# Other SBUF addresses for the operands of the split-float32 matmuls of a hybrid decoder layer

## The chip, the cores and the metric

One core of one Trainium2 chip. The metric is the device time of one execution in microseconds; the median of three runs of the kernel before is 854.86 us (854.53 to 857.35).

## What is computed

A decoder layer in float32 on 256 tokens of width 1024: a SwiGLU block (FFN1), a mixer in which a Mamba-2 branch and a retention branch run side by side, a second SwiGLU block (FFN2), each with a norm and a modulation from a conditioning vector, and a last norm. Cut to what matters:

```
u = modulate(rms_norm(h, norm_ffn1_w), sh1, sc1)
h = h + 0.5 * g1 * (silu(u @ w_gate) * (u @ w_up)) @ ffn1_w_out      # 1024 -> 2 x 2816 -> 1024
u = modulate(rms_norm(h, norm_mix_w), sh2, sc2)
z, xbc, dt, q, k, v, g, gates = split(u @ mix_w_in)                  # 1024 -> 13344
h = h + g2 * (gate_s * (ssd(z, xbc, dt) @ w_br_ssd)
            + gate_r * (retention(q, k, v, g) @ w_br_ret)) @ mix_w_out
u = modulate(rms_norm(h, norm_ffn2_w), sh3, sc3)
h = h + 0.5 * g3 * (silu(u @ w_gate2) * (u @ w_up2)) @ ffn2_w_out
out = rms_norm(h, norm_final_w)
```

## The kernel before

Activations lie transposed: features on the 128 partitions, the 256 tokens along the row. Every large projection is done as three matmuls with operands that are split into two parts (`float32r`): a high part, rounded by ScalarE's cast, and a low part, which VectorE gets by subtracting the high part from the full value. `mm3` (L138 to L141) issues high x high (L139), low x high (L140) and high x low (L141) into the same PSUM sum. In nearly all of them a piece of 128 x 128 weights is loaded into TensorE and 256 tokens of an activation stream past it. Where this text says "streamed operand" it means the one that flows through, and "weights" the one that is loaded; the profile writes `proj<-uh,wh` for "uh streams past wh into proj".

The tiles by name:

- `wst` holds weights as they come from memory by DMA (four buffers of 8 KB a partition), `wh` and `wl` their high and low parts (four buffers of 4 KB each, L130 and L131 in `half`).
- `uh` and `ul` are the parts of the normed and modulated activation u: eight rows of 256 tokens, with 320 elements from row to row (`U_ROW`), and two more columns that `modulated` uses (258 columns in its matmuls).
- `s` tiles are the mixer's slots: 17 buffers of 4 KB that hold, among others, the split results of both branches, which stream past `w_br_ssd`, `w_br_ret` and `mix_w_out`.
- `ah` and `al` are the split products of a SwiGLU block, which stream past the weights of its second projection in FFN1 (`contract`).
- In the v columns of the mixer (`v_tile`) and in the last projection (`ffn2_w_out`, from L985 on) the roles are changed: activations are loaded, and `wh` and `wl` stream, with 512 columns or 256.
- The narrow projection for dt (L577 to L582) puts both parts of its weights into one `wh` buffer and loads 64 or 32 columns of it at a time.

Weights arrive on SyncE's DMA queue in the order of use. In the first phase (up to the first part of FFN1's first projection) the order of ScalarE, VectorE and TensorE is written out by hand (`manual_schedule`); in the rest the code's order stands, and a list of steps (`ORDER`) sets that of the mixer.

Where a tile lies in a partition follows from the pools: `cst`, then `wp` (wst, wh, gap, wl), then `sp` (am, g, eb, gap, uh, ul and small tiles), and after these a pool for each phase, which holds `ah` and `al` or the slots. Nothing but the sizes of what stands ahead sets an address. A tile `gap` in `wp` and one in `sp` hold no data; they only move what follows. The sizes of u's rows, of the weights' pieces and of all buffers named above are multiples of 256 bytes, so that all rows of a tile have the same address modulo 256.

## Time and profile before

| | |
|---|---|
| median of three runs | 854.86 us (854.53 to 857.35) |
| the profiled execution | 856.98 us, span 854.9 us |
| TensorE busy, weight loads busy | 842.5 us, 816.4 us |
| VectorE, ScalarE, GpSimd busy | 667.5, 519.2, 10.3 us |
| mean granted TensorE clock | 0.998 |
| moved by DMA | 193.14 MB, 226 GB/s in the mean |

Matmuls overlap: one lasts some 0.28 us from start to modelled end, while the next starts about 0.12 us after it. Their rate is read from starts, or from a count in a stretch of time, and not from the mean duration. A matmul of plain float32 stands as two records in the trace, one of `float32r` as one.

### The profile page before, as it was taken

What the parts mean: (1) busy time and instruction counts of PE and PEld (TensorE: products, weight loads), DVE (VectorE), ACT (ScalarE), POOL (GpSimd) and SP (SyncE); (2) the same over time, 40 slices, a digit from 0 to 9 for tenths busy, and PEclk for the clock granted to TensorE, in tenths of its full rate; (3) what the DMA queues carried; (4) which work ended last, traced back from release to release, by engine and by line L of the source; (5) the groups of instructions that cost most, each with busy time, mean ns of one, the idle gap of its engine ahead of it and who ended that gap; (6) DMA issues with size and microseconds to landing.
All of it is one profiled execution on the core that took longest, in us unless ns stands there. A gap on an engine that the chain in (4) does not pass through costs nothing.

```text
span 854.9 us, 16219 instructions
## 1 busy us (share of the span) xinstructions
PE 842.5 (99%) x6734; PEld 816.4 (95%) x6734; DVE 667.5 (78%) x1002; ACT 519.2 (61%) x743; POOL 10.3 (1%) x21
## 2 busy tenths in 40 slices
PE   8999999999999999999999999999999999999996
PEld 6999999999999989899999999999999999999896
DVE  6989979886989987687898777977979975455463
ACT  6665544465798686766465568765558644545342
POOL 0000000000100010000000000000000000000000
PEclk9999999999999999999999999999999999999999
DMA  9987889984595455446657662645555685455521
GB/s 371 422 316 263 289 293 349 362 321 149 203 323 195 169 210 199 142 153 227 225 180 294 247 241 105 212 183 185 212 195 201 250 311 198 150 188 176 189 89 49
DMA packets 30587, 193.14 MB, mean 226 GB/s; under 512 B 3489, under 2 KB 4129, under 8 KB 10034
## 3 DMA queue, kind: packets, MB, share of 16 engines
q1 hardware_dynamic: 28656, 186.40, 59.6%
q0 software_dynamic: 1568, 5.28, 1.9%
q8 instruction: 52, 0.85, 0.4%
q10 hardware_dynamic: 290, 0.44, 0.1%
q14 instruction: 21, 0.17, 0.1%
HBM read 191.02 MB, written 1.08 MB: 225 GB/s over the span
## 4 chain that ended last, share of the span: by engine, by line
PE 91%; issue 4%; DMA 2%; ACT 2%; DVE 1%; DVEq 0%; ACTq 0%; POOLq 0%
PE proj L139 28%; PE proj L141 27%; PE proj L140 27%; PE misc L139 1%; PE misc L141 1%; PE misc L140 1%; DMA k<-in_consts_dram 1%; DMA m<-rows 1%; PE misc L734 1%; PE misc L207 1%; PE misc L878 1%; ACT wh L130 0%; DMA h<-in_x_dram 0%; PE misc L744 0%; ACT s L171 0%
## 5 line engine op out<-in xcount | busy, mean ns | idle before, releaser
L130 ACT CAST wh<-wst 128x1024 fp32r<-128x1024 f32 (+1 forms) x263 | 273.2, 1040 | 252.7 <-PE proj L140 166.8
L131 DVE TENSOR_TENSOR wl<-wst,wh 128x1024 fp32r<-128x1024 f32 (+1 forms) x263 | 317.3, 1210 | 128.7 <-ACT wh L130 128.0
L139 PE MATMUL proj<-uh,wh 128*128 128x256 f32 (+1 forms) x1312 | 369.3, 281 | 0.0
L141 PE MATMUL proj<-uh,wl 128*128 128x256 f32 (+1 forms) x1312 | 368.0, 280 | 0.0
L140 PE MATMUL proj<-ul,wh 128*128 128x256 f32 (+1 forms) x1312 | 367.5, 280 | 0.0
L141 PEld LDWEIGHTS proj<-uh,wl 128*128 128x128 f32 x1312 | 248.2, 189 | 0.2 <-issue 0.2
L139 PEld LDWEIGHTS proj<-uh,wh 128*128 128x128 f32 x1312 | 247.1, 188 | 0.3 <-ACT wh L130 0.2
L140 PEld LDWEIGHTS proj<-ul,wh 128*128 128x128 f32 x1312 | 246.9, 188 | 0.3 <-issue 0.2
L139 PE MATMUL proj<-s,wh 128*128 128x256 f32 x320 | 90.2, 283 | 1.0 <-ACT s L800 0.8
L141 PE MATMUL proj<-s,wl 128*128 128x256 f32 x320 | 89.6, 280 | 0.0
L140 PE MATMUL proj<-s,wh 128*128 128x256 f32 x320 | 89.5, 280 | 0.0
L183 DVE SCALAR_TENSOR_TENSOR wst<-wst,cb 128x1024 f32<-128x1024 f32 x56 | 67.0, 1221 | 3.3 <-DMA wst<-in_ada_w_dram 3.3
L139 PEld LDWEIGHTS proj<-s,wh 128*128 128x128 f32 x320 | 60.0, 188 | 2.1 <-ACT s L800 1.7
L141 PEld LDWEIGHTS proj<-s,wl 128*128 128x128 f32 x320 | 60.5, 189 | 0.0
L140 PEld LDWEIGHTS proj<-s,wh 128*128 128x128 f32 x320 | 60.1, 188 | 0.0
L139 PE MATMUL proj<-ah,wh 128*128 128x256 f32 x176 | 49.5, 281 | 0.0
L140 PE MATMUL proj<-al,wh 128*128 128x256 f32 x176 | 49.4, 281 | 0.0
L141 PE MATMUL proj<-ah,wl 128*128 128x256 f32 x176 | 49.4, 281 | 0.0
L139 PE MATMUL proj<-wh,ah 128*128 128x256 f32 (+1 forms) x132 | 42.1, 319 | 0.0
L140 PE MATMUL proj<-wl,ah 128*128 128x256 f32 (+1 forms) x132 | 42.0, 318 | 0.0
L141 PE MATMUL proj<-wh,al 128*128 128x256 f32 (+1 forms) x132 | 41.8, 317 | 0.0
L163 ACT ACT_TABLE_LOAD x30 | 38.5, 1283 | 1.2 <-PEq L1040 0.7
(247 smaller groups left out, 1132.6 us busy)
## 6 DMA issues: line engine op xcount, KB each, us to landing
wst<-in_mix_w_in_dram SPq DMA_DIRECT2D x52, 1024.0 KB, 4.9
wst<-in_ffn_w_in_dram SPq DMA_DIRECT2D x43, 1024.0 KB, 6.5
wst<-in_ada_w_dram SPq DMA_DIRECT2D x28, 1024.0 KB, 6.2
wst<-in_ffn_w_out_dram SPq DMA_DIRECT2D x17, 1024.0 KB, 5.2
ada<-in_ada_w_dram SPq DMA_DIRECT2D x16, 512.0 KB, 12.2
wst<-in_w_br_ssd_dram SPq DMA_DIRECT2D x8, 1024.0 KB, 5.2
wst<-in_w_br_ret_dram SPq DMA_DIRECT2D x8, 1024.0 KB, 4.9
wst<-in_ffn_w_out_dram SPq DMA_DIRECT2D x6, 768.0 KB, 4.5
```

Source lines behind the costliest of these rows:

```text
L130: act.copy(hi, v)
L131: dve.tensor_tensor(lo, v, hi.bitcast(F32), ALU.subtract)
L139: pe.matmul(o, l[0], r[0], start=first, stop=False, skip_group_check=skip)
L140: pe.matmul(o, l[0], r[1], start=False, stop=False, skip_group_check=skip)
L141: pe.matmul(o, l[1], r[0], start=False, stop=last, skip_group_check=skip)
L163: ins = act.preload_act_table_set(name).ins
L183: dve.scalar_tensor_tensor(st[:, i, :], st[:, i, :], 1.0, cb, ALU.mult, ALU.mult, accum_out=raw[:, j, f0 + i:f0 + i + 1])
L207: pe.matmul(ps[:, :T], mean, s, start=i == 0, stop=i == len(parts) - 1)
L734: pe.matmul(py[hh * 64:hh * 64 + 64, f * T + c * P:f * T + (c + 1) * P], xd[:, c, hl * 64:hl * 64 + 64], m[c][:, hl, :], start=True, stop= ...
L878: pe.matmul(py[:, eh, :], v[:, 0, es], sc[:, :T], start=True, stop=False)
```

## The change

No instruction is added, taken away or moved. Tiles get other addresses, and two tiles are read at an offset in a larger buffer:

- a `wh` buffer has 64 elements more, and its data begin 46 elements in (`WH_AT`), or 8 elements in where it streams in the last projection (`WH_MOVING`);
- the gap ahead of `wl` shrinks from 16 to 8 elements and the gap ahead of `uh` from 48 to 40;
- `ah` and `al` of FFN2 begin 48 and 0 elements into their buffers instead of 24 and 16.

Addresses modulo 256 bytes, from the two programs' allocations:

| | before | after |
|---|---|---|
| uh, ul | 0 | 192 |
| slots | 0 | 192 |
| ah, al in FFN1 | 0 | 192 |
| wh | 96 | 24 |
| wl | 160 | 128 |
| last projection: wh, wl | 96, 160 | 128, 128 |
| last projection: ah, al | 96, 160 | 128, 128 |

Smaller tiles that come after these in a partition move along.

```diff
+WH_AT, WH_MOVING = 46, 8
...
-    for tag, n, bufs in (("am", KD, 2), ("g", KD, 2), ("eb", 4, 1), ("gap", 48, 1)):
+    for tag, n, bufs in (("am", KD, 2), ("g", KD, 2), ("eb", 4, 1), ("gap", 40, 1)):
...
-    def half(v):
+    def high_weights(at_=WH_AT):
+        t = wp.tile([P, 1024 + 64], F32R, tag="wh", name=nm("wh"), bufs=HALF_BUFS)
+        return t[:, at_:at_ + 1024]
+
+    def low_weights():
+        return wp.tile([P, 1024], F32R, tag="wl", name=nm("wl"), bufs=HALF_BUFS)
+
+    def half(v, at_=WH_AT):
         nk, n = v.shape[1], v.shape[2]
-        hi = wp.tile([P, 1024], F32R, tag="wh", name=nm("wh"), bufs=HALF_BUFS)
-        lo = wp.tile([P, 1024], F32R, tag="wl", name=nm("wl"), bufs=HALF_BUFS)
+        hi, lo = high_weights(at_), low_weights()
...
-            his = [wp.tile([P, 1024], F32R, tag="wh", name=nm("wh"), bufs=HALF_BUFS) for _ in range(2)]
+            his = [high_weights() for _ in range(2)]
             if kt == 0:
-                wp.tile([P, 16], F32, tag="gap", name="wgap")
-            los = [wp.tile([P, 1024], F32R, tag="wl", name=nm("wl"), bufs=HALF_BUFS) for _ in range(2)]
-            return his, los
+                wp.tile([P, 8], F32, tag="gap", name="wgap")
+            return his, [low_weights() for _ in range(2)]
...
-            wd = wp.tile([P, 1024], F32R, tag="wh", name=nm("wh"), bufs=HALF_BUFS)
-            wd = wd[:, :KD * 2 * NH].rearrange("p (k n) -> p k n", k=KD)
+            wd = high_weights()[:, :KD * 2 * NH].rearrange("p (k n) -> p k n", k=KD)
...
-                   .rearrange("p (f t) -> p f t", f=NF) for name, n in (("ah", 24), ("al", 16)))
+                   .rearrange("p (f t) -> p f t", f=NF) for name, n in (("ah", 48), ("al", 0)))
...
-                hvs = [half(st[:, k2:min(k2 + per // 2, kn), :]) for k2 in range(0, kn, per // 2)]
+                hvs = [half(st[:, k2:min(k2 + per // 2, kn), :], WH_MOVING) for k2 in range(0, kn, per // 2)]
```

## The prediction

> **What bounds the kernel now.** I read the page's busy times first, then its chain, then the costliest groups, then stretches of the span, and last single instructions in order of time.

> ```profile
> span 854.9 us, 16219 instructions
> PE 842.5 (99%) x6734; PEld 816.4 (95%) x6734; DVE 667.5 (78%) x1002; ACT 519.2 (61%) x743; POOL 10.3 (1%) x21
> ...
> PE 91%; issue 4%; DMA 2%; ACT 2%; DVE 1%; DVEq 0%; ACTq 0%; POOLq 0%
> ...
> L139 PE MATMUL proj<-uh,wh 128*128 128x256 f32 x1280 | 359.9, 281 | 0.0
> L139 PE MATMUL proj<-s,wh 128*128 128x256 f32 x320 | 90.2, 283 | 1.0 <-ACT s L800 0.8 <-ACT s L135 0.2
> L139 PE MATMUL proj<-ah,wh 128*128 128x256 f32 x176 | 49.5, 281 | 0.0
> L139 PE MATMUL misc<-uh,wh 128*128 128x256 f32 x64 | 18.0, 281 | 0.0
> L139 PE MATMUL proj<-wh,ah 128*128 128x256 f32 x88 | 24.7, 281 | 0.0
> L139 PE MATMUL proj<-wh,uh 128*128 128x512 f32 x64 | 26.1, 408 | 0.0
> L139 PE MATMUL proj<-wh,ah 128*128 128x512 f32 x44 | 17.4, 395 | 0.0
> L139 PE MATMUL proj<-uh,wh 128*128 128x258 f32 x32 | 9.4, 294 | 0.0
> L139 PE MATMUL misc<-uh,wh 128*128 128x258 f32 x32 | 9.1, 283 | 0.0
> ```

> TensorE is busy 99% and is 91% of the chain; its largest groups wait 0.0 to 1.0 us in all. So the time is the number of matmuls times the spacing of their starts. Each L139 row has a twin at L140 and one at L141, so there are 3 x (1280 + 320 + 176 + 64 + 88) = 5784 matmuls with 256 columns, 3 x (64 + 44) = 324 with 512 and 3 x (32 + 32) = 192 with 258. The mean of 281 ns is no spacing, because matmuls overlap. The spacing comes from stretches that hold little else: length by count. The columns after the stretch are its length, TensorE's busy time with the count, weight loads, VectorE, ScalarE and GpSimd where shown, the granted clock, the share of DMA and GB/s.

> ```profile
> 20.00:203.00 183.00, 183.00 (x1549) 1.00 0.83 314
> 229.00:286.00 57.00, 57.00 (x496) 1.00 0.69 241
> 325.00:334.00 9.00, 9.00 (x80) 1.00 0.52 170
> 359.00:368.00 9.00, 9.00 (x81) 1.00 0.40 129
> 392.00:407.00 15.00, 15.00 (x132) 1.00 0.58 187
> 429.00:500.00 71.00, 71.00 (x617) 1.00 0.64 229
> 672.00:724.00 52.00, 52.00 (x442) 1.00 0.74 267
> 789.00:816.00 27.00, 27.00 (x118) 1.00 0.54 178
> 820.00:846.00 26.00, 26.00 (x223) 1.00 0.09 31
> ```

> A stretch also counts matmuls that began before it and still run: 0.28 us over a spacing near 0.117 is 2.4 of them. Without these, 20 to 203 us gives 183 / 1546.6 = 118.3 ns and 672 to 724 us 118.3 ns, but 229 to 286 us gives 57 / 493.6 = 115.5 ns and 429 to 500 us 115.5 ns. These are the same instruction on the same tiles at the same places, with the clock at 1.00 in all rows. So there are two gaits, 115.5 and 118.3 ns, and neither DMA (0.83 beside 0.09) nor the clock separates them. The five stretches of the fast gait are 161 us, or 161 / 0.1155 = 1394 matmuls. The last projection runs at 26 / 220.6 = 117.9 ns (its 264 matmuls with 256 columns) and 27 / 116.3 = 232.2 ns (with 512, where 0.39 us of overlap is 1.7 matmuls). The other 5784 - 1394 - 264 = 4126 run in the slow gait. The mean over the 5784 is 117.6 ns.

> **The change part by part.** It adds, removes and moves no instruction and no wait; each engine has the same list in the same order. Only addresses differ. The costs are these.

> *Places of the streamed operand and of the weights.* Before, u, the slots and the FFN1 activations stand at 0 modulo 256 and are streamed against weights at 96 and 160. Now they stand at 192, against 24 and 128; in the last projection weights and activations go from 96 and 160 to 128. That touches every row above. No row shows the new places, so the spacing has to be bounded by the nearest rows:

> ```profile
> 207.47 0.28 PE L139 MATMUL misc<-uh,wh 128*128 128x258 f32 x1
> ...
> 216.35 0.28 PE L141 MATMUL misc<-uh,wl 128*128 128x258 f32 x1
> ...
> 828.53 0.29 PE L139 MATMUL proj<-wh,ah 128*128 128x256 f32 x1
> 828.66 0.28 PE L140 MATMUL proj<-wl,ah 128*128 128x256 f32 x1
> ...
> 829.95 0.27 PE L139 MATMUL proj<-wh,ah 128*128 128x256 f32 x1
> 830.06 0.28 PE L140 MATMUL proj<-wl,ah 128*128 128x256 f32 x1
> ```

> From above: the first two rows are 74 matmuls apart, 8.88 / 74 = 120.0 ns for 258 columns, or 119.1 ns for 256. That is the worst gait in this trace. From below: single matmuls in the last projection take 0.11 us to the next one and others 0.13 us, at the same two pairs of places. So one matmul can be done in 0.110, if the stall that hits it falls elsewhere.

> What I take is 115.5 ns for all of it: the best spacing that this trace holds over hundreds of matmuls, with weights at places that differ from those of u, as they still do. Working: 4126 x 2.8 ns = 11.6 us from the slow gait, 264 x 2.4 ns = 0.6 us from the last projection, 192 x (120.0 - 116.4) ns = 0.7 us from the 258-column matmuls and 324 x (232.2 - 231.0) ns = 0.4 us from those with 512. The sum is 13.3 us.
> The ends: at 110 ns it is 5784 x 7.6 = 44.0, 324 x 12.2 = 4.0 and 192 x 9.1 = 1.7 us, so 49.7 us less. At 119.1 ns it is 1394 x 3.6 + 4126 x 0.8 + 264 x 1.2 ns = 8.6 us and 324 x 6.0 ns = 1.9 us, so 10.5 us more. I lean to the gain because the kernel now stands near the upper end: 4126 of 5784 matmuls pay 118.3 out of 110 to 119.1.

> [...]

> *Casts and subtractions into the moved tiles.*

> ```profile
> L130 ACT CAST wh<-wst 128x1024 fp32r<-128x1024 f32 (+1 forms) x263 | 273.2, 1040 | 252.7 <-PE proj L140 166.8 <-issue 38.0 <-PE proj L141 34.8
> L131 DVE TENSOR_TENSOR wl<-wst,wh 128x1024 fp32r<-128x1024 f32 (+1 forms) x263 | 317.3, 1210 | 128.7 <-ACT wh L130 128.0
> ...
> 50.00:100.00 50.00, 50.00 (x424) 50.00 (x424) 46.98 (x73) 28.25 (x37) 0.00 (x0) 1.00 0.77 279
> ```

> I cost these at nothing. ScalarE idles 252.7 us ahead of its casts, mostly for TensorE, and VectorE 128.7 us for ScalarE. If each took a 32nd longer (8.5 and 9.9 us), the idle time would still cover it. The cover is thinnest in FFN1: of 50 us from 50 to 100, VectorE works 46.98. At 115.5 ns TensorE needs 48.8 us for that stretch, so VectorE stays hidden. Below about 111 ns it would not, and what TensorE then saved in the first 200 us would be given back there. That is a further reason not to take the lower end.

> **The rivals.**
> *A gait better than any stretch shows.* If the stall falls outside most matmuls, say 113 ns, halfway between 110 and 115.5: 5784 x 4.6 + 324 x 6.2 + 192 x 6.1 ns = 29.8 us, 825 us. For it: single matmuls at 0.11. Against it: no stretch shows it.

> [...]

> *The fast gait is lost.* If the new places have only the slow gait, 1394 x 2.8 ns = 3.9 us more, 859 us; with 119.1 ns, 865 us. For it: two gaits at equal places mean that what goes before a stretch picks the gait, and any new place draws again.

> *Nothing, or part of it.* If the places don't matter at all and only the way into a stretch does, the same order of instructions leads to the same gaits and 855 us. If some stretches turn fast and others stay, 846 to 852 us.

> **How the numbers follow.** The profiled execution took 856.98 us beside its span of 854.9; the median of the three runs is 854.86, 2.1 us less, so the sum is taken off the median as off the span: 854.86 - 13.3 = 841.6 us. Chances: this forecast (832 to 846) 0.40, a better gait (below 832) 0.25, part of it 0.08, nothing 0.07, fast gait lost 0.10, load sets the pace 0.10. That is faster 0.73, within 0.3% (2.6 us, about what a measurement of this kernel can tell) 0.07, slower 0.20. The range runs from 816 to 863: below lies the part of the better gait under 112 ns, some 0.06, above mainly the load, some 0.12. The forecast's own range is 832 to 846.

> **What the changed profile would show.** Right: the same counts, with stretches of FFN1 (20 to 203 us) and FFN2 holding 1.024 times the matmuls per microsecond, near 115.5 ns, and the last projection near 231 ns with 512 columns. The granted clock and the waits of the L139 groups stay as they are. [...] VectorE's limit would show as idle time of TensorE after L131 in FFN1. What would make the prediction wrong is a spacing for u at 192 outside 113 to 118 ns, since every microsecond hangs on that one number: 1 ns is 5.8 us.

## The result, and the profile after

| | before | after |
|---|---|---|
| median of six runs each | 855.32 us (854.53 to 857.35) | 842.34 us (837.63 to 847.19) |
| ratio of the times | | 0.985, 95% interval 0.981 to 0.989 |
| profiled execution, its span | 856.98, 854.9 us | 843.66, 841.1 us |

The forecast of 841.6 us is 0.7 us from the median. Two things were not forecast: the six runs of the kernel after scatter over 9.6 us (five later ones over 3.5) where the six of the kernel before lie within 2.8 (and eleven later ones within 6.7), and, as the rows below show, the sum is made of other terms.

First the page of the kernel after: its busy times, the shares of its chain, and four of the costliest groups.

```profile
span 841.1 us, 16219 instructions
PE 826.0 (98%) x6734; PEld 798.9 (95%) x6734; DVE 665.9 (79%) x1002; ACT 516.3 (61%) x743; POOL 10.3 (1%) x21
...
PE 77%; DVE 7%; DMA 7%; issue 5%; ACT 3%; DVEq 0%; ACTq 0%; POOLq 0%
...
L137 ACT CAST wh<-wst 128x1024 fp32r<-128x1024 f32 (+1 forms) x263 | 271.6, 1038 | 221.9 <-PE proj L147 123.4
L138 DVE TENSOR_TENSOR wl<-wst,wh 128x1024 fp32r<-128x1024 f32 (+1 forms) x263 | 316.8, 1209 | 113.8 <-ACT wh L137 113.1
L146 PE MATMUL proj<-uh,wh 128*128 128x256 f32 (+1 forms) x1312 | 365.3, 278 | 0.0
...
L146 PEld LDWEIGHTS proj<-uh,wh 128*128 128x128 f32 x1312 | 246.7, 188 | 0.3 <-ACT wh L137 0.2
```

The counts are the same. A cast takes 1038 ns (1040 before), a subtraction 1209 (1210) and a weight load 188 (188): neither the engines that write the moved tiles nor the loads from them changed by more than 2 ns in the mean. TensorE's share of the chain has fallen from 91% to 77%, and what took its place is DMA and VectorE. The loads before, beside the last of the rows above:

```profile
L139 PEld LDWEIGHTS proj<-uh,wh 128*128 128x128 f32 x1312 | 247.1, 188 | 0.3 <-ACT wh L130 0.2
```

Now the stretches. The columns are length, TensorE's busy time with its count, clock, DMA share and GB/s; from the count 2.4 are taken off as before (1.7 with 512 columns).

```profile
59.00:137.00 78.00, 78.00 (x691) 1.00 0.80 300
140.00:200.00 60.00, 58.67 (x504) 1.00 0.83 309
227.00:279.00 52.00, 52.00 (x461) 1.00 0.74 260
446.00:490.00 44.00, 44.00 (x390) 1.00 0.69 255
661.00:710.00 49.00, 49.00 (x415) 1.00 0.76 276
776.00:800.00 24.00, 24.00 (x108) 1.00 0.52 183
806.00:829.00 23.00, 23.00 (x194) 1.00 0.11 35
```

FFN1 runs at 78 / 688.6 = 113.3 ns where it ran at 118.3, and the mixer's stretches at 113.4 and 113.5. But the first half of FFN2's first projection runs at 49 / 412.6 = 118.8 ns, the last projection's matmuls with 256 columns at 23 / 191.6 = 120.0 (117.9 before), and those with 512 at about 226 (232.2). In the row from 140 to 200 us, FFN1's second projection, TensorE is busy for 58.67 of 60 us; it has begun to wait.

Since every matmul of one trace has its twin in the other, the difference of the spans can be put together from the starts. A gap over 1.7 times the median counts as a wait; of it, what is above the median stands in the last column.

| matmuls | count | spacing before, after (ns) | difference (us) | of it, longer waits |
|---|---|---|---|---|
| 256 columns, not in the last projection | 5520 | 117.55, 114.30 | -14.8 | +3.2 |
| 258 columns | 192 | 120.0, 119.1 | +0.6 | +0.7 |
| 512 columns, v | 192 | 235.1, 235.3 | 0.0 | 0.0 |
| 512 columns, last projection | 132 | 231.2, 226.9 | -0.6 | 0.0 |
| 256 columns, last projection | 264 | 117.7, 120.0 | +0.6 | 0.0 |
| all others, start and tail | | | +0.4 | |
| sum | | | -13.8 | |

The waits of ScalarE between 138 and 212 us tell where most of the 3.2 us comes from (total, times, longest); first the kernel before, then the kernel after.

```profile
ACT wh L130 <- PE proj L140: 22.9, 15, 2.0
ACT wh L130 <- DMA wst<-in_ffn_w_out_dram: 4.4, 3, 3.3
```

```profile
ACT wh L137 <- DMA wst<-in_ffn_w_out_dram: 13.5, 7, 4.5
ACT wh L137 <- PE proj L147: 5.9, 4, 1.9
...
PE proj L148 <- DVE wl L138: 1.2, 3, 0.6
```

Before, the cast of the next weights mostly waited for TensorE to free a buffer: weights were early. After, it mostly waits for the weights themselves, at a DMA share of 0.83, as in FFN1 before. The last line is TensorE's: it now waits for VectorE's low part (L138), which needs the cast, which needs the weights; in the kernel before TensorE has no wait here. Eight gaps of 0.2 to 0.9 us between the starts of matmuls, 2.4 us in all above the spacing, fall into this projection, which took 62.96 us instead of 62.48. Between two of them, one of 0.9 us at 155 us and one of 0.4 us at 169 us, the matmuls ran in a slower gait, at 9 / 75.6 = 119.0 ns, and before and after at 113.3; that is another 0.6 us:

```profile
157.00:166.00 9.00, 9.00 (x78) 1.00 0.93 325
```

### The profile page after: what moved, and what is told of

It reads as the page before. It is cut to its first block, busy times and chain, and to the rows that moved or that the text cites. A ratio compares the mean times of both kernels' runs of the same rounds, so it can differ in the third digit from the quotient of the medians.

```text
span 841.1 us, 16219 instructions
## 1 busy us (share of the span) xinstructions
PE 826.0 (98%) x6734; PEld 798.9 (95%) x6734; DVE 665.9 (79%) x1002; ACT 516.3 (61%) x743; POOL 10.3 (1%) x21
## 4 chain that ended last, share of the span: by engine, by line
PE 77%; DVE 7%; DMA 7%; issue 5%; ACT 3%; DVEq 0%; ACTq 0%; POOLq 0%
PE proj L146 23%; PE proj L147 23%; PE proj L148 23%; DMA wst<-in_ada_w_dram 4%; DVE wl L138 3%; DVE wst L190 2%; PE misc L147 1%; PE misc L146 1%; PE misc L148 1%; ACT wh L137 1%; DMA k<-in_consts_dram 1%; DMA wst<-in_ffn_w_out_dram 1%; DMA m<-rows 1%; PE misc L739 1%; PE misc L883 1%
## 5 line engine op out<-in xcount | busy, mean ns | idle before, releaser
L137 ACT CAST wh<-wst 128x1024 fp32r<-128x1024 f32 (+1 forms) x263 | 271.6, 1038 | 221.9 <-PE proj L147 123.4
L138 DVE TENSOR_TENSOR wl<-wst,wh 128x1024 fp32r<-128x1024 f32 (+1 forms) x263 | 316.8, 1209 | 113.8 <-ACT wh L137 113.1
L146 PE MATMUL proj<-uh,wh 128*128 128x256 f32 (+1 forms) x1312 | 365.3, 278 | 0.0
L148 PE MATMUL proj<-uh,wl 128*128 128x256 f32 (+1 forms) x1312 | 363.9, 277 | 0.1
L146 PE MATMUL proj<-s,wh 128*128 128x256 f32 x320 | 89.1, 280 | 1.2 <-ACT s L805 0.8
L147 PE MATMUL proj<-s,wh 128*128 128x256 f32 x320 | 88.4, 277 | 0.0
L147 PE MATMUL proj<-al,wh 128*128 128x256 f32 x176 | 48.8, 277 | 0.0
L146 PE MATMUL proj<-ah,wh 128*128 128x256 f32 x176 | 48.8, 277 | 0.0
```

The source lines that it names most:

```text
L137: act.copy(hi, v)
L138: dve.tensor_tensor(lo, v, hi.bitcast(F32), ALU.subtract)
L146: pe.matmul(o, l[0], r[0], start=first, stop=False, skip_group_check=skip)
L147: pe.matmul(o, l[0], r[1], start=False, stop=False, skip_group_check=skip)
L148: pe.matmul(o, l[1], r[0], start=False, stop=last, skip_group_check=skip)
```

## The experiments

Two theories were to be told apart. The first: the spacing follows from the distance, modulo 256 bytes, between the operand that streams and the weights (the address of the weights less that of the streamed operand). The second: it follows from where one of the two stands by itself. Beside them stood the question of what picks the gait at equal places.

**Stages, for all kernels.** Microseconds between the starts of the same two matmuls in the profiled executions; mm is the number of matmuls. The numbers over the columns are those of the experiments below.

| stage | before | after | after, second profile (8) | 2, streamed moved | 2, weights moved | 3 | 5 | 6 | 7 | 8 |
|---|---|---|---|---|---|---|---|---|---|---|
| FFN1 first projection, start (384 mm) | 46.6 | 45.2 | 45.2 | 46.3 | 46.0 | 45.6 | 45.2 | 46.0 | 45.7 | 45.7 |
| its rest (672) | 79.5 | 76.2 | 76.2 | 80.6 | 79.7 | 76.2 | 76.2 | 79.2 | 79.9 | 77.7 |
| FFN1 second projection (528) | 62.5 | 63.0 | 63.2 | 63.4 | 62.6 | 60.5 | 62.3 | 62.2 | 62.8 | 61.0 |
| mixer (3168) | 437.9 | 429.7 | 431.4 | 446.5 | 442.5 | 430.9 | 430.7 | 433.9 | 433.2 | 433.0 |
| FFN2 first projection (960) | 117.1 | 115.1 | 115.1 | 118.6 | 117.3 | 115.0 | 115.1 | 114.8 | 112.5 | 112.5 |
| last projection, 512 columns (132) | 30.5 | 30.0 | 30.0 | 30.5 | 30.0 | 30.0 | 30.5 | 30.8 | 29.9 | 30.5 |
| last projection, 256 columns (263) | 31.0 | 31.6 | 31.6 | 31.0 | 31.6 | 31.6 | 29.8 | 31.0 | 31.6 | 29.8 |
| median of the runs | 855.3 | 842.3 | 843.6 | 869.1 | 860.9 | 840.9 | 841.8 | 849.8 | 842.1 | 839.9 |

**1. Matmuls alone.** A program that computes nothing of the layer: 83 stretches of 48 `float32r` matmuls, each stretch with its own places, and a short matmul ahead of each (of 64 columns, or of the number given as the way in).

```diff
+ for mvs, sts, n, m, way in segments():          # places, columns, loaded columns, way in
+     pe.matmul(ps[:, :way], ones, ones[:, :way], start=True, stop=True)
+     for i in range(48):
+         mo = 32 + 512 * (i % 4) + mvs[i % len(mvs)] // 4
+         so = 32 + 256 * (i % 8) + sts[i % len(sts)] // 4
+         pe.matmul(ps[:m, :n], st[:, so:so + m], mv[:, mo:mo + n], ...)
```

> A kernel of matmuls alone: 85 stretches of 48 matmuls, each after one short float32 matmul, with the streamed operand and the weights at chosen places modulo 256; it computes none of the layer. Theory 'distance': the spacing follows the distance from streamed operand to weights, so streamed 0 with weights 88 gives the same as 192 with 24, the sweep over 0 and the sweep over 192 agree at each distance, and between distances it moves from about 113.3 to about 120 ns; the way in gives two values at some of them. Rival 'own place': the two sweeps differ at equal distance. Rival 'load length': 64 and 32 loaded columns are spaced closer than 128. Rival 'smooth cost': from 240 to 272 columns the spacing grows by 0.42 to 0.47 ns a column; theory 'steps' says it stays on whole multiples of 6.67 ns (106.7, 113.3, 120.0) wherever it is settled.

Eight stretches, each from the start of its 13th matmul to that of its 48th, which is 35 spacings. In this order: streamed 0 against weights 64, 96 and 160; streamed 192 against 96; 32 loaded columns at 0 against 96; the kernel before's set (0 against 96, 96, 160 in turn), entered after 64 columns and after 96; the kernel after's distances (0 against 88, 88, 192).

```profile
66.05:70.02 3.97, 3.97 (x38) 1.00 0.00 0
...
89.42:93.53 4.11, 4.11 (x38) 1.00 0.00 0
...
136.87:141.07 4.20, 4.20 (x37) 1.00 0.00 0
...
284.27:288.47 4.20, 4.20 (x37) 1.00 0.00 0
...
378.01:382.13 4.12, 4.12 (x37) 1.00 0.00 0
383.87:387.91 4.04, 4.04 (x37) 1.00 0.00 0
389.67:393.80 4.13, 4.13 (x37) 1.00 0.00 0
...
418.67:422.63 3.96, 3.96 (x37) 1.00 0.00 0
```

Divided by 35, with the starts to the nanosecond, they are 113.3, 117.3, 120.1; 120.1; 117.8; 115.5 and 118.3; 113.3 ns. What follows:

- The distance decides. Streamed 192 against 96 is 160 apart, modulo 256, and behaves like 0 against 160. Seven of the eight distances that were tried from 0 and from 192 agree within 0.1 ns by the same way in; 64 apart gave 113.3 from 0 and 117.8 from 192. (At distance 0 this is the settled spacing, 120.0 ns: it was the program's first stretch, and its first matmuls start 213 ns apart.)
- Loading 32 or 64 columns instead of 128 changes the spacing by 0.5 ns at most, and not with the length (117.8 and 117.1 ns beside 117.3), so it isn't the length of the load.
- The two gaits of the kernel before, 115.5 and 118.3 ns, come back with nothing but matmuls in the program, after 64 columns the one, after 96 and 128 the other.
- Over all distances from 0 to 248 in steps of 8 the settled spacing lies between 113.3 and 120.1 ns. No stretch with 256 columns was below 113.3.
- It isn't the distance to the weights of the next matmul, whose load starts within 0.01 us of the stream in the traces of before and after (both at 66.28 us in the one). The last projection's set before (96, 160, 96 streamed past 96, 96, 160 in turn) would then be at distance 0 throughout, like 128 against 128. It runs at 117.6 to 118.0 ns with 256 columns and 231.2 with 512, equal places at 120.0 and 226.7. The distances to each matmul's own weights (0, 192, 64) leave room for that; which load matters is not shown beyond this.

**2. The two halves of the change apart.** Two kernels: the streamed operands alone at 192 (distances 160 and 224 to the weights), and the weights alone at 24 and 128 (distances 24 and 128).

```diff
  # before.py
-    for tag, n, bufs in (("am", KD, 2), ("g", KD, 2), ("eb", 4, 1), ("gap", 48, 1)):
+    for tag, n, bufs in (("am", KD, 2), ("g", KD, 2), ("eb", 4, 1), ("gap", 96, 1)):
...
-  for name, n in (("ah", 24), ("al", 16)))
+  for name, n in (("ah", 40), ("al", 16)))
```

> The kernel before with u, slots and FFN1 activations moved to 192 alone; weights stay at 96 and 160, the last projection as before. If the place of the streamed operand does it by itself: long stretches at 113.3 ns and about 842 us. If the place of the weights does it: 115.5 and 118.3 ns and 855 us, as before. Theory 'distance': a third pair of distances (160 and 224 instead of 96 and 160 before, 88 and 192 after), so neither of the two sets of gaits.

```diff
  # after.py
-    for tag, n, bufs in (("am", KD, 2), ("g", KD, 2), ("eb", 4, 1), ("gap", 40, 1)):
+    for tag, n, bufs in (("am", KD, 2), ("g", KD, 2), ("eb", 4, 1), ("gap", 56, 1)):
...
-  for name, n in (("ah", 48), ("al", 0)))
+  for name, n in (("ah", 32), ("al", 0)))
```

> The changed kernel with u, slots and FFN1 activations back at 0; weights at 24 and 128, the last projection as after. If the place of the weights does it by itself: 113.3 ns and about 842 us. If that of the streamed operand does it: 115.5 and 118.3 ns and about 855 us. Theory 'distance': distances 24 and 128, again new gaits and not those of either kernel.

FFN1 and FFN2 of the first kernel, then of the second:

```profile
20.00:200.00 180.00, 180.00 (x1503) 1.00 0.85 316
...
682.00:734.00 52.00, 52.00 (x435) 1.00 0.73 269
```

```profile
20.00:200.00 180.00, 180.00 (x1521) 1.00 0.86 320
...
676.00:728.00 52.00, 52.00 (x441) 1.00 0.74 265
```

The first is 869.14 us, ratio 1.016 (1.012 to 1.020), at 180 / 1500.6 = 120.0 ns and about as much in all stages but the last projection, where its places are those of before; the second 860.85 us, 1.007 (1.005 to 1.009), at 118.5 ns. Either half of the change alone makes the kernel slower; only both together make it faster. So neither operand's place brings the gain by itself, and the thin cover of the casts has no part in the loss: it is the spacing, and FFN1's second projection has no gap between its matmuls in either kernel.

**3. Everything moved by 64 bytes.** All places of the kernel after plus 64, with the same distances.

```diff
-WH_AT, WH_MOVING = 46, 8
+WH_AT, WH_MOVING = 62, 24
...
-                wp.tile([P, 8], F32, tag="gap", name="wgap")
+                wp.tile([P, 24], F32, tag="gap", name="wgap")
```

> Everything of the changed kernel moved on by 64 bytes: u, slots and FFN1 activations at 0, wh at 88, wl at 192, in the last projection all at 192. All distances are those of the changed kernel, all places others. Theory 'distance': 113.3 ns in most stretches, 226.7 and 120.0 ns in the last projection, 838 to 847 us. Rivals 'own place' of either operand: other gaits, 850 us or more.

```profile
60.00:136.00 76.00, 76.00 (x673) 1.00 0.84 308
...
659.00:712.00 53.00, 53.00 (x448) 1.00 0.75 266
```

840.85 us, ratio 0.983 (0.979 to 0.987), with FFN1 at 76 / 670.6 = 113.3 and FFN2's first half at 53 / 445.6 = 118.9 ns: the gaits of the kernel after, as also in the last projection; in the mixer 144 matmuls of `mix_w_out` and some smaller groups were slow that were fast there (see experiment 8). With experiments 1 and 2 this settles that it is the distance.

**4. More columns, distances and ways in.** The program of matmuls alone again, with 512 and 258 columns at 16 distances, and 15 ways in from 16 to 128 columns for two sets of places.

> Matmuls alone again (none of the layer is computed): distances in steps of 16 bytes for 512 and for 258 columns, distances around 64 in steps of 4 bytes for 256 columns, and 15 ways in (16 to 128 columns of a short matmul) for two sets of weights, all at distance 64 and in turn at 88, 88, 192. Theory 'distance with gaits': 512 columns run at 226.7 ns at distance 0 and at 228 to 236 ns elsewhere; 88, 88, 192 settles at 113.3 ns from most ways in and at 118.9 ns from some, distance 64 at 113.3 ns from all. Rival 'the way in does not matter': one spacing for all 15 ways in both sets.

With 512 columns, equal places settled at 226.7 ns (227.8 with the slow start of the program's very first stretch), and all other distances gave 228.3 to 234.3 (the first program had 226.7 for 128 against 128 and 231.0 for the distances 88, 88, 192). With 256 columns, 128 against 128 had 120.0 there from all three ways in. So equal places are the best that was found for 512 columns and among the worst for 256: the last projection's change holds one of each. With 258 columns the range is 117.8 to 122.2, and 119.2 for the kernel after's distances. In steps of 4 bytes with 256 columns, 52 and 64 gave 113.3 ns, and 56, 60, 68 and 72 gave 117.7 to 119.4, so the neighbours of 64 are not good. Both sets, 64 and (88, 88, 192), stayed at 113.3 from all 15 ways in; here the program of matmuls alone did not show the slow gait that the layer has at 88, 88, 192.

**5. The last projection by the same distances.** Its weights stay at 128 as they stream; the loaded activations go from 128 to 216 and 64.

```diff
-  for name, n in (("ah", 48), ("al", 0)))
+  for name, n in (("ah", 6), ("al", 24)))
```

> The changed kernel with the last projection's activations at 216 and 64 instead of 128 (weights that stream there stay at 128), so that its distances are 88 and 192, as in the other stages. Theory 'distance': its 256-column matmuls go from 120.0 to 113.3 ns (264 x 6.7 ns = 1.8 us less), its 512-column ones from 226.7 to 231.1 ns (132 x 4.4 ns = 0.6 us more), 1.2 us less in all, about 841 us. Rival 'equal places are best where weights stream': the 256-column matmuls don't gain.

The stretches with 512 and with 256 columns:

```profile
775.00:802.00 27.00, 27.00 (x119) 1.00 0.54 180
806.00:829.00 23.00, 23.00 (x206) 1.00 0.11 35
```

With 256 columns it runs at 23 / 203.6 = 113.0 ns instead of 120.0 (29.8 us instead of 31.6), with 512 at 231 instead of 227 (30.5 instead of 30.0). The stage gains 1.2 us; the whole, 841.80 us with ratio 0.985 (0.983 to 0.987), can't be told from the kernel after.

**6. One distance of 64 for all.** Simpler than the change under study, and without offsets in the weights' buffers: the streamed operand at 32, both halves of the weights at 96.

```diff
  # before.py
-    for tag, n, bufs in (("am", KD, 2), ("g", KD, 2), ("eb", 4, 1), ("gap", 48, 1)):
+    for tag, n, bufs in (("am", KD, 2), ("g", KD, 2), ("eb", 4, 1), ("gap", 72, 1)):
...
-            if kt == 0:
-                wp.tile([P, 16], F32, tag="gap", name="wgap")
...
-  for name, n in (("ah", 24), ("al", 16)))
+  for name, n in (("ah", 32), ("al", 0)))
```

> The kernel before with one distance for all: u, slots and FFN1 activations at 32, wh and wl at 96, in the last projection weights at 96 and activations at 160, so each load stands 64 bytes above what streams. Theory 'distance': 113.3 ns from every way in, also in FFN2's first half and in the last projection's 256 columns, so 2.5 + 1.8 us less than the changed kernel, 837 to 839 us, and runs that scatter less. Rival 'three loads in turn are needed': 116 to 120 ns and 850 us or more.

```profile
20.00:140.00 120.00, 120.00 (x1021) 1.00 0.86 326
229.00:285.00 56.00, 56.00 (x496) 1.00 0.72 247
```

849.79 us, ratio 0.993 (0.990 to 0.995). FFN1 stayed at 120 / 1018.6 = 117.8 ns and the first stretch of the mixer at 56 / 493.6 = 113.5. The expectation of one gait fell: 113.3 and 117.8 were the two values that the first program had found for this distance from two places, and 15 of 15 ways in at 113.3 in the second did not mean that the layer would get it. Here the layer has both at the same places, within one execution. FFN2's first half and the last projection's 256 columns were to gain as well: they ran at 117.8 ns, and only FFN2's second half, from 739 us on, at 113.3.

**7. A short matmul on the way in.** If what goes ahead of a stretch picks its gait, one more short matmul in front of FFN2's second step should pick again.

```diff
+                if p2 == 1:
+                    ps = misc_ps()
+                    pe.matmul(ps[:, :64], ones, ones[:, :64], start=True, stop=True)
```

> The changed kernel with one more short float32 matmul (64 columns, its result is not used) ahead of FFN2's second pair of tiles, where the 258-column matmuls end. All places as after. Theory 'gaits': what goes before a stretch picks its gait, so FFN2's first half may go from 118.9 to 113.3 ns, 460 x 5.6 ns = 2.6 us less, less 0.2 us for the matmul itself. Rival 'places alone set the gait': it stays at 118.9 ns and the time is 0.2 us longer.

FFN2's first projection fell from 115.1 to 112.5 us, 2.6 us for the 480 matmuls that left the slow gait (480 x 5.6 ns = 2.7). The whole is 842.11 us, ratio 0.985 (0.980 to 0.991), with runs at 837.94, 838.22, 846.00 and 848.07 us. In the slowest of these, which is the profiled one, FFN1 had the slow gait:

```profile
20.00:140.00 120.00, 120.00 (x1012) 1.00 0.86 325
```

120 / 1009.6 = 118.9 ns, in a program that up to there is the kernel after, instruction by instruction. FFN1 took 4.0 us more than in the profile of the kernel after and the mixer 3.5. It isn't the chip: the kernel of experiment 5, which has the same places in FFN1, had the fast gait there on the same one. So places and instructions do not fix the gait by themselves; what a stretch comes in with matters, and then the gait lasts to the next break, as it did in FFN1's second projection after. These 7.5 us make it likely that the gait is also what divides the four times into two near 838 and two near 847 us; that is not shown, since only one of them was profiled.

**8. All of it, and the kernel after once more.** The places of experiment 5 and a short matmul at five places (in FFN1's first projection at its seventh step, twice in FFN1's second, at the start of `mix_w_out`, and in FFN2), beside a further profile of the kernel after.

```diff
+    def nudge():
+        ps = misc_ps()
+        pe.matmul(ps[:, :64], ones, ones[:, :64], start=True, stop=True)
...
+            if f2 == 0 or (f2 == 2 and nk > 8):
+                nudge()
...
+            if p2 == 6:
+                nudge()
...
+                if p2 == 1:
+                    nudge()
```

> The places of the run with the last projection's distances at 88 and 192, and five short float32 matmuls (64 columns, results not used): in FFN1's first projection ahead of its third late pair of tiles, ahead of the first and the third pair of FFN1's second projection, ahead of mix_w_out and ahead of FFN2's second pair. Theory 'gaits drawn at the way in': FFN1's stretches run at 113.3 ns in every execution from the first of these on, FFN2's first half and mix_w_out too. Against the changed kernel 2.6 (FFN2) + 1.2 (last projection) + 0.8 (mix_w_out) - 5 x 0.2 us = 3.6 us less where FFN1 had the fast gait anyway, and up to 4 us more than that where it had the slow one: 836 to 840 us, with less scatter than 838 to 847. Rival 'the way in only matters in FFN2': 840 to 845 us and the scatter stays.

> The changed kernel once more, on the same chip as the run beside it, for its scatter and for the gait that FFN1 takes in another execution. Theory 'gaits drawn at the way in': its runs spread from 837 to 848 us, and the stretches of FFN1 or of the mixer that run at 118.9 ns are others than in the first profile. Rival 'places alone set the gait': the same stretches at the same spacing, and the scatter has another source.

FFN1's first projection ahead of the short matmul and behind it, then FFN2's first half:

```profile
20.00:82.00 62.00, 62.00 (x524) 1.00 0.88 342
90.00:150.00 60.00, 60.00 (x531) 1.00 0.84 315
...
663.00:714.00 51.00, 51.00 (x453) 1.00 0.76 279
```

This execution drew 62 / 521.6 = 118.9 ns in FFN1, and changed to 60 / 528.6 = 113.5 at the short matmul. Experiment 7's execution, with the same instructions in FFN1 but for the short matmuls, kept 118.9 ns to the end of FFN1. So the short matmul, or the break that it makes, ended the slow gait. FFN2 has 113.2. But the mixer's first long stretch, 504 matmuls, drew 56 / 470.6 = 119.0 ns this time:

```profile
225.00:281.00 56.00, 56.00 (x473) 1.00 0.72 245
```

The median is 839.91 us, the lowest of all kernels here, ratio 0.983 (0.981 to 0.986); the kernel after beside it took 843.57, 0.987 (0.985 to 0.990). The intervals touch, so the further 3.7 us are likely and not proven. Less scatter was expected than the 837 to 848 us of the kernel after: these five runs lie within 4.8 us, and the kernel after's own five beside them within 3.5, so neither its expected spread nor the gain in scatter was seen. In its second profile the kernel after had the slow gait again in FFN2's first half, at 53 / 445.6 = 118.9 ns, and this time also in 144 matmuls of `mix_w_out`, which had been fast in the first:

```profile
661.00:714.00 53.00, 53.00 (x448) 1.00 0.75 268
```

Over the six profiles with these distances (the kernel after twice, experiments 3, 5, 7 and 8), stretches differ in how they draw. FFN2's first half was slow in all four without a short matmul ahead and fast in both with one. `mix_w_out` was slow in four of five without one. FFN1 and the mixer's first long stretch were fast in four and slow in experiments 7 and 8.

The ways in differ by little where the draw differs. The first two matmuls of that long stretch start 230 ns apart in the four fast profiles and 222 in the two slow ones. At the start of FFN1 the split matmuls (or those ahead of them) first start 213 ns apart, until the spacing falls at once to about half, 14 to 18 us into the span; the granted clock reads 1.00 throughout. In experiments 7 and 8 this happens at about the first split matmul, in the kernel after and experiment 5 at the fourth, in the second profile at the tenth, and in experiment 3 ahead of all. That this moment picks FFN1's gait fits the profiles and is not shown.

## Why the prediction came out right, step by step

- **What bounds the kernel** held. TensorE stays at 98%, and every stage that changed did so by the spacing of its matmuls, but for 3.9 us of waits (3.2 and 0.7 in the table).
- **115.5 ns for all** had the right mechanism, places that change the spacing, and the wrong number. It took the best gait of the trace for the new places as well. But each set of distances has gaits of its own, for this one 113.3 and 118.9 ns, and 114.3 in the mean. The 5520 matmuls gained 3.25 ns each where the forecast had 2.1, or 11.6 us for all; that is some 18 us, of which 3.2 went to waits, and 14.8 are left.
- **That 841.6 came within 0.7 us of 842.34 is luck.** The spacing of the 5520 brought 6.4 us more than forecast. Against that stand 3.9 us of waits that the forecast put at nothing, and some 2 us by which the other rows of the table fell short. Even that the places would help was no more than a lean: nothing in the trace said that this set is better than its two halves, which lose. The forecast's own sign of being wrong, a spacing outside 113 to 118 ns, is there in FFN2's first half, at 118.9.
- **The upper end, 119.1 ns,** was too low: 120.0 exists, and the streamed operands' half of the change alone has it. **The lower end, 110 ns,** is not reached: it was read from single matmuls of 0.11 us, which are part of a pattern. In the slow gait of the kernel before, the gaps of twelve matmuls in a row (119, 118, 117, 118, 122, 120, 118, 119, 120, 116, 116, 117 ns) come again every 1420 ns. Only the sum over such a pattern is a rate.
- **The last projection** was sized at a gain of 0.6 us for 256 columns; it lost 0.6. The 0.4 us for 512 columns were spread over all 324; the 192 in the v columns run at 235 ns before and after and gained nothing, the 132 of the last projection gained 0.6: equal places lose on the one and gain on the other.
- **258 columns**: 0.7 us forecast, by spacing 0.9 ns x 192 = 0.2 us, and a longer wait at one entry took it back. In the other profile of the kernel after that wait is not there.
- **Casts at nothing** held for their durations. The cover in FFN1 was seen to be thin, but VectorE was named as next and a limit near 111 ns. At 113.3 ns the named sign came, TensorE waiting for VectorE's subtraction (1.2 us, L138), but what the casts ahead of it waited for most was the DMA of FFN1's second weights (13.5 us of ScalarE's waits instead of 4.4); TensorE lost 2.4 us. In experiments 3 and 5, whose distances in FFN1 are the same, this projection took 60.5 and 62.3 us, so the price scatters. In experiment 3 ScalarE waited 14.6 us for the same DMA and TensorE's gaps came to 0.6, so that wait alone does not give the price.
- **The load that sets the pace** (0.10, and the main part of the 0.12 above the range): no run shows a load that the new places lengthen. Loads still take 188 ns, and 32 loaded columns give the spacing of 128 within 0.5 ns. **That places don't matter** (0.07) is refuted by 869.14 and 860.85 us beside 840.85: the distance between the two operands moves the spacing of 256 columns from 113.3 to 120.0 ns.
- **A better gait** (0.25, 825 us at 113 ns) was right on the number for most stretches and wrong on its reach: FFN2's half and other slow stretches, the waits and the last projection keep the time at 842.
- The range's scatter was not foreseen: the forecast spoke of gaits that the way in picks, but took them as fixed by the program.

What stays open: why these distances give these spacings; why the layer has 118.9 ns at distances for which the program of matmuls alone settles at 113.3 from every way in; what makes the small differences at the way in between two executions; and how much of the 9.6 us of scatter they account for.

## What to carry to other kernels

In this kernel, with TensorE busy for 98% of the span, the places of its two operands moved the spacing of 256 columns between 113.3 and 120.0 ns. Where TensorE is the bound elsewhere, treat them as a parameter like the tile size: sweep the distance modulo 256 bytes in a program of matmuls alone, for each number of columns by itself (equal places had 226.7 ns with 512 columns, the lowest found, and 120.0 with 256, among the highest), and then look at the stretches of the real kernel: the set that had 113.3 ns from all 15 ways in alone also ran at 118.9 in the layer. When a stage gets faster, read at once what its feeder waits for (here 13.5 us for the DMA of FFN1's second weights instead of 4.4). And where single runs scatter more than before (9.6 us here instead of 2.8), compare medians and profile more than one execution before a stage's gain is believed.
